# Sums of weight quarters on GpSimd, copies ahead of weighings, and a last product in column halves: a fast matrix product on one core

## Chip, cores, metric

One core of one Trainium2 chip. The metric is the device time of one execution in microseconds (us), as the median of several. The kernel before took 1509.08 us (four runs, 1508.4 to 1509.49), the changed kernel is compared with it below.

## The reference

```python
def reference(x, w):            # x: 8 x 2048 x 2048, w: 2048 x 2048, float32
    cs = np.cumsum(x, axis=1)
    diff = cs - np.concatenate([zeros, cs[:, :-1, :]], axis=1)   # = x up to rounding
    return np.matmul(diff, w).astype(np.float32)
```

The kernel computes x w: 16384 rows by 2048 by 2048. Rows come in tiles of 128, four tiles in a group.

Of the kernel before, what the change touches and what calls it, by code (L numbers as in the profile page):

```python
# [33 lines left out]
def kernel(  # L34
# [6 lines left out]
    nc = tc.nc  # L41
    P = 128
# [7 lines left out]
    NB = 512  # L50
# [3 lines left out]
    ADD = mybir.AluOpType.add  # L54
    SUB = mybir.AluOpType.subtract
    MUL = mybir.AluOpType.mult
    MAX = mybir.AluOpType.max
    AX = mybir.AxisListType
# [75 lines left out]
    def after(engine, ask):  # L134
        if engine in last:
            with tc.issue_after(last[engine].ins):
                said = ask()
        else:
            said = ask()
        last[engine] = said[-1] if isinstance(said, tuple) else said  # L140
        return said


    with tc.tile_pool(name="ring", bufs=7) as ring, tc.tile_pool(
# [97 lines left out]
        def put(c, rows, columns, queue=nc.gpsimd):  # L242
            return queue.dma_start(out2[rows, columns], c)
# [102 lines left out]
        got = {}  # L346
# [130 lines left out]
    def product_in(ps, a, b, first):  # L477
        for k in range(4):
            nc.tensor.matmul(  # L479
                ps, a[k], b[k], start=(first and k == 0), stop=(k == 3), skip_group_check=True  # L480
            )
# [13 lines left out]
    def keep(dst, ps, scale):  # L495
        for c, p in pieces_of(dst, ps):
            after("act", lambda: nc.scalar.activation(c, p, COPY, scale=scale))  # L497
# [12 lines left out]
    def total(dst, p, q, op):  # L510
        after("dve", lambda: nc.vector.tensor_tensor(dst.all, p.all, q.all, op))  # L511

    def less(dst, p, q):
        for k in range(len(dst)):
            after("dve", lambda: nc.vector.tensor_tensor(dst[k], p[k], q[k], SUB))  # L515


    def less_in(Q1, Q2, Q4, t11, t12, t21, t22):
        less(Q1, t12, t11)
        less(Q2, t22, Q1)  # L520
        less(Q4, t21, Q2)

    def less_in3(Q1, Q2, Q4, t11, t12, t21, t22):
        less(t12, t22, t12)

    def new_c(slot):
        return cpool.tile([P, NH], f32, name=f"c{slot}")
# [5 lines left out]
    def fetch_x(t):  # L533
        if t < END:
            came[t], _ = after("sp", lambda: bring(t))

    def weigh(t, slot):
        if t < END:
            xf = came.pop(t)
            m, _ = after("act", lambda: measure(xf, new_c(slot)))  # L540
            got[t] = m, None, xf


    def weigh_in(t, ps):
        if t < END:
            xf = came.pop(t)
            m = small.tile([P, 1], f32, name="m")
            m4 = small.tile([P, 4], f32, name="m4")
            for i in range(4):
                at = ds(i * NB, NB)  # L550
                after(
                    "act",
                    lambda: nc.scalar.activation(  # L553
                        ps[i % 2],
                        xf[:, at],
                        ABS,
                        scale=1.0 / ROW,
                        accum_out=m4[:, i : i + 1],
                    ),
                )  # L560
            after("dve", lambda: nc.vector.tensor_reduce(m, m4, AX.X, ADD))  # L561
            got[t] = m, None, xf

    def scale_of(t):
        if t < END:
            m, _, xf = got[t]
            s, _ = after("dve", lambda: invert(m))
            came[t] = xf, s

# [77 lines left out]
    def group_plain(g, X, Y, Z, V, a, b, c, d):  # L647
        h = g + 2
        ug, uh = unit(g), unit(h)
        A11g, A12g = parts(g)  # L650
        A11h, A12h = parts(h)
        A21g, A22g = parts(g + 1)
        product(X, A11g, B11, True)
        for k in range(3):
            block(B22, 1, 1, k, "act")
        C11g = new_c(a)
        keep(C11g, X, ug)
        for k in range(3, KH):
            block(B22, 1, 1, k, "act" if k < 6 else "dve")
        product(V, A12g, B21, True)  # L660
        product(Y, A11h, B11, True)
        add(C11g, V, ug)
        put(C11g, g, 0)

        less(T3[:2], B22[:2], B12[:2])
        total(S1, A21g, A22g, ADD)
        product(Z, A12h, B21, True)
        weigh(h + 1, d)
        C11h = new_c(b)
        keep(C11h, Y, uh)  # L670
        total(S2, S1, A11g, SUB)
        less(T2[:4], B22[:4], T1[:4])
        scale_of(h + 1)
        vg = unit(g + 1)
        ready(h + 1)
        turn(h + 1)
        fetch_x(h + 4)
        less(T2[4:], B22[4:], T1[4:])
        product(V, S1, T1, True)
        C22 = new_c(d)  # L680
        keep(C22, V, vg)
        less(T3[2:3], B22[2:3], B12[2:3])
        total(S4g, A12g, S2, SUB)
        product(X, S2, T2, False)
        C12g = new_c(c)
        keep(C12g, X, ug)
        total(A21g, A11g, A21g, SUB)
        less(T3[3:], B22[3:], B12[3:])
        product(V, S4g, B22, False)
        A21h, A22h = parts(h + 1)  # L690
        vh = unit(h + 1)
        weigh(g + 4, a)
        product(X, A21g, T3, False)
        total(S1, A21h, A22h, ADD)
        total(S2, S1, A11h, SUB)
        add(C11h, Z, uh)
        put(C11h, h, 0)
        scale_of(g + 4)
        ready(g + 4)
        turn(g + 4)  # L700
        add(C12g, V, ug)
        put(C12g, g, 1)
        fetch_x(g + 5)
        product(Y, S2, T2, False)
        C12h = new_c(a)
        keep(C12h, Y, uh)
        add(C22, X, vg)
        put(C22, g + 1, 1)
        total(S4h, A12h, S2, SUB)
        less(T4, B21, T2)  # L710
        product(Z, S1, T1, True)
        total(A21h, A11h, A21h, SUB)
        weigh(h + 4, b)
        scale_of(h + 4)
        ready(h + 4)
        turn(h + 4)
        fetch_x(h + 5)
        weigh(g + 5, c)
        scale_of(g + 5)
        C22 = new_c(d)  # L720
        keep(C22, Z, vh)
        product(X, A22g, T4, False)
        C21 = new_c(b)
        keep(C21, X, vg)
        ready(g + 5)
        turn(g + 5)
        put(C21, g + 1, 0)
        product(Y, A21h, T3, False)
        add(C22, Y, vh)
        put(C22, h + 1, 1)  # L730
        less_in(*in2)
        less_in3(*in2)
        product(Z, S4h, B22, False)
        add(C12h, Z, uh)
        put(C12h, h, 1)
        fetch_x(g + 8)
        less_in(*in3)
        product(Y, A22h, T4, False)
        C21 = new_c(c)
        keep(C21, Y, vh)  # L740
        put(C21, h + 1, 0)

    def group(g, X, Y, Z, V, a, b, c, d):
# [9 lines left out]
            units[g], units[h] = unit(g), unit(h)  # L753
        u = ug, uh = units.pop(g), units.pop(h)

        C11g = new_c(a)
        keep(C11g, X, ug)
        S3g = sums(g, S4g)
        if second:
            weigh(h + 1, c)  # L760
            ready(h + 1)
            less_in(*in4)
        turn(h + 1)
        fetch_x(h + 4)
        product(Y, A11h, B11, True)
        if second:
            weigh_in(g + 4, V)
        C11h = new_c(b)
        keep(C11h, Y, uh)
        if not second:  # L770
            weigh_in(g + 4, V)
        scale_of(g + 4)
        vg, vh = unit(g + 1), unit(h + 1)
        A21h, A22h = parts(h + 1)
        product(X, S2, T2, False)
        C12g = new_c(c)
        keep(C12g, X, ug)
        one, two, A2 = sums_in(A12g, A12h, S4h, S0)
        one()
        two()  # L780
# [5 lines left out]
        total(A21h, A11h, A21h, SUB)  # L786
        total(S2, S1, A11h, SUB)
        S3h = A21h
        product(X, S3g, T3, False)
        add(C22, X, vg)  # L790
        put(C22, g + 1, 1)
# [11 lines left out]
                ready(h + 4)  # L803

        inner_product(A2, in2, banks, C11g, C11h, *u, between_2)
        if second:
            less_in3(*in3)
            less_in3(*in4)
        total(S4h, A12h, S2, SUB)
        turn(h + 4)  # L810
        put(C11h, h, 0)
# [60 lines left out]
        def four_last():  # L872
            a11, a12, a22, s1, s2, s3, s4 = A4
            Q1, Q2, Q4, t11, Q3, t21, t22 = in4
            C21g, C21h = new_c(b), new_c(c)
            product_in(q, a11, t11, True)
            keep(C21g[:, :NB], q, vg)
            product_in(X[0], a12, t21, False)
            add(C21g[:, :NB], X[0], vg)
            product_in(X[1], s4, t22, False)  # L880
            keep(C21g[:, NB:], X[1], vg)
            product_in(e, s1, Q1, True)
            add(C21g[:, NB:], e, vg)
            keep(C21h[:, NB:], Y[1], vh)
            add(C21h[:, NB:], e, vh)
            product_in(q, s2, Q2, False)
            add(C21g[:, NB:], q, vg)
            put(C21g, g + 1, 0)
            product_in(Y[0], a22, Q4, False)
            keep(C21h[:, :NB], Y[0], vh)  # L890
            product_in(q, s3, Q3, False)
            for n in range(2):
                at = ds(n * NB, NB)
                add(C21h[:, at], q, vh)
                nc.scalar.dma_start(out2[ds((h + 1) * P, P), at], C21h[:, at])

        inner_product(A3, in3, banks, C12g, C12h, *u, between_3)
        put(C12h, h, 1)
# [43 lines left out]
```

## The kernel before: what the change touches

Products are cut by a scheme that uses seven products for eight (with sums of quarters of x and of w) on two levels, in fp16 with a scale a row. TensorE makes products into PSUM banks. ScalarE *weighs* a row tile (sum of absolute values, for its scale), *narrows* it to fp16 (`ready`), and copies the first product of a bank pair out (`keep`). VectorE adds further products (`add`) and makes the sums of x (`sums`, `total`) and of w (`less`). `in2`, `in3`, `in4` are the inner sums of three quarters of w, 12 in `less_in` and 4 in `less_in3` each; they are made once, from the end of the first group (`group_plain`) into the second. `after` keeps the order of instructions on each engine.

```python
def less(dst, p, q):
    for k in range(len(dst)):
        after("dve", lambda: nc.vector.tensor_tensor(dst[k], p[k], q[k], SUB))
# ... end of group_plain (a, b, c, d are slots of the output buffer c) ...
    less(T4, B21, T2)
    product(Z, S1, T1, True)
    weigh(h + 4, b); scale_of(h + 4); ready(h + 4)      # (cut)
    weigh(g + 5, c)
    scale_of(g + 5)
    C22 = new_c(d)
    keep(C22, Z, vh)
    product(X, A22g, T4, False)                         # (cut: keep of X)
    product(Y, A21h, T3, False)
    add(C22, Y, vh)
    less_in(*in2); less_in3(*in2)
    product(Z, S4h, B22, False)
    add(C12h, Z, uh)
    less_in(*in3)
    product(Y, A22h, T4, False)
# ... start of the second group (inside `group`, second == True) ...
    product(X, A11g, B11, True)
    keep(C11g, X, ug)
    S3g = sums(g, S4g)                                  # sums of x, on VectorE
    weigh(h + 1, c); ready(h + 1)
    less_in(*in4)
    product(Y, A11h, B11, True)
    weigh_in(g + 4, V)                                  # in four pieces, waste into PSUM
    keep(C11h, Y, uh)
    product(X, S2, T2, False)
    keep(C12g, X, ug)
    product(Z, S1, T1, True)
    keep(C22, Z, vg)
    # ... inner_product(A2, in2, ...), then:
    less_in3(*in3); less_in3(*in4)
```

## Time and profile before

| | before |
|---|---|
| median time | 1509.08 us |
| TensorE busy, of the span | 1490.6 of 1507.3 us |
| VectorE, ScalarE, GpSimd busy | 1104.4, 864.5, 5.2 us |
| matmuls (all but 64 of 512 columns); one of 512 | 6911; 0.216 us |
| end of the last matmul to the end of the span | 4.9 us |

TensorE is the bound: whatever is gained must come out of the few microseconds in which it stands still. The prediction shows the lines for that.

### The profile page before, as it was taken

Reading aid. Unit: us, or ns where it says so; the run is one execution under the profiler, and the core shown is the slowest. Engines: PE = TensorE matmul, PEld = TensorE weight load, DVE = VectorE, ACT = ScalarE, POOL = GpSimd, SP = SyncE. Lnnn points to the kernel's source line nnn. Section 1 sums busy time; section 2 is a strip of 40 time slices with the busy share of each in tenths; the row PEclk is TensorE's granted clock in tenths of the full one; section 3 lists DMA queues with packets and bytes.
Section 4 is the critical chain, followed back from the end, with each engine's and each line's share of the span. In section 5 each row is a group of like instructions: output and inputs, shape, how many; then the busy total and the mean of one; then the engine's idle time right before and its main releaser. Section 6 shows DMA issues by size and latency. Waiting matters only on the chain.

```text
span 1507.3 us, 19123 instructions
## 1 busy us (share of the span) xinstructions
PE 1490.6 (99%) x6911; PEld 673.8 (45%) x6911; DVE 1104.4 (73%) x2053; ACT 864.5 (57%) x1107; POOL 5.2 (0%) x12
## 2 busy tenths in 40 slices
PE   8999999999999999999999999999999999999998
PEld 3444444444444444444444444444444444444443
DVE  7997777776677676777676776766776767776767
ACT  5875655565655566555656555655555565556551
POOL 0100000000000000000000000000000000000000
PEclk9999999999999999999999999999999999999999
DMA  9988878878978987888789788878788888887772
GB/s 362 351 250 233 236 224 246 234 213 227 235 225 244 224 224 236 215 246 236 210 229 232 230 241 217 235 222 248 216 244 207 236 221 250 232 236 216 223 208 112
DMA packets 322479, 351.50 MB, mean 233 GB/s; under 512 B 266896, under 2 KB 266896, under 8 KB 306512
## 3 DMA queue, kind: packets, MB, share of 16 engines
q1 hardware_dynamic: 321536, 347.92, 81.1%
q0 software_dynamic: 560, 1.84, 0.3%
q8 instruction: 54, 0.88, 0.2%
q10 hardware_dynamic: 288, 0.52, 0.1%
q14 instruction: 41, 0.34, 0.1%
HBM read 150.99 MB, written 134.22 MB: 189 GB/s over the span
## 4 chain that ended last, share of the span: by engine, by line
PE 88%; DVE 1%; DMA 1%; issue 0%; ACT 0%; DVEq 0%; ACTq 0%; SPq 0%
PE b L468 52%; PE b L479 36%; DVE c L502 1%; DMA fin<-in_x_dram 0%; DMA xT<-fin 0%; DVE W L511 0%; ACT b L553 0%; DVE W L515 0%; ACT c L497 0%; DVEq L937 0%; DVE xT L511 0%; DVE s L112 0%; DVE m L111 0%; DVE u L586 0%; DVE m L561 0%
## 5 line engine op out<-in xcount | busy, mean ns | idle before, releaser
L502 DVE SCALAR_TENSOR_TENSOR c<-b,u,c 128x512 f32<-128x512 f32 (+1 forms) x883 | 675.0, 799 | 234.8 <-ACT c L497 112.8
L497 ACT ACTIVATE c<-b,u 128x512 f32<-128x512 f32 x496 | 314.5, 680 | 265.4 <-PE b L468 170.5
L468 PE MATMUL b<-W,xT 128*128 128x512 f16 x2048 | 462.1, 379 | 0.8 <-ACT c L497 0.8
L468 PE MATMUL b<-W,W 128*128 128x512 f16 x1764 | 411.7, 379 | 1.8 <-ACT c L497 1.5
L105 ACT ACTIVATE c<-fin 128x2048 f16<-128x2048 f32 x92 | 175.7, 1910 | 242.4 <-DMA out_dram<-c 220.5
L468 PEld LDWEIGHTS <-xT 128*128 128x128 f16 x2048 | 200.4, 98 | 242.6 <-issue 1.1
L468 PEld LDWEIGHTS <-W 128*128 128x128 f16 x2016 | 197.2, 98 | 240.2 <-issue 2.1
L116 ACT ACTIVATE fin<-fin,s 128x2048 f16<-128x2048 f32 x123 | 246.3, 2002 | 93.8 <-issue 50.8
L479 PEld LDWEIGHTS <-W 128*128 128x128 f16 x1560 | 152.1, 98 | 187.5 <-issue 2.5
L479 PE MATMUL b<-W,W 128*128 128x512 f16 x810 | 220.0, 379 | 1.0 <-DVE c L502 1.0
L479 PE MATMUL b<-W,xT 128*128 128x512 f16 x720 | 180.0, 379 | 0.0
L479 PE MATMUL b<-inner,W 128*128 128x512 f16 x660 | 176.2, 379 | 0.0
L479 PEld LDWEIGHTS <-xT 128*128 128x128 f16 x960 | 93.9, 98 | 113.3
L561 DVE TENSOR_REDUCE m<-m 128x1 f32<-128x4 f32 x29 | 4.6, 157 | 106.7 <-ACT b L553 106.7
L553 ACT ACTIVATE b<-fin 128x512 f32<-128x512 f32 x116 | 67.8, 585 | 14.5 <-DMA fin<-in_x_dram 14.5
L468 PE MATMUL b<-W 128*128 128x512 f16 x252 | 75.0, 379 | 0.0
L511 DVE TENSOR_TENSOR W<-W,xT 128x1024 f16<-128x1024 f16 x122 | 68.2, 559 | 3.2
L511 DVE TENSOR_TENSOR W<-xT,W 128x1024 f16<-128x1024 f16 x122 | 67.5, 553 | 0.0
L479 PE MATMUL b<-inner,xT 128*128 128x512 f16 x240 | 61.6, 379 | 0.0
L233 PE MATMUL b<-wb,xP 128*128 128x512 bf16 x240 | 55.4, 383 | 5.9 <-ACT wb L216 4.8
L511 DVE TENSOR_TENSOR W<-xT,xT 128x1024 f16<-128x1024 f16 (+1 forms) x92 | 54.8, 596 | 0.0
L111 DVE TENSOR_SCALAR m<-m 128x1 f32<-128x1 f32 x124 | 18.5, 149 | 34.6 <-ACT c L105 33.5
(54 smaller groups left out, 457.9 us busy)
## 6 DMA issues: line engine op xcount, KB each, us to landing
out_dram<-c SPq DMA_DIRECT2D x247, 512.0 KB, 3.1
fin<-in_x_dram SPq DMA_DIRECT2D x123, 1024.0 KB, 5.5
W<-in_w_dram SPq DMA_DIRECT2D x32, 512.0 KB, 9.6
W<-in_x_dram SPq DMA_DIRECT2D x16, 256.0 KB, 7.4
xT<-fin SPq DMA_TRANSPOSE x184, 5.2
out_dram<-o POOLq DMA_DIRECT2D x7, 256.0 KB, 3.9
out_dram<-o SPq DMA_DIRECT2D x7, 256.0 KB, 4.1
xP<-in_x_dram SPq DMA_DIRECT2D x1, 1024.0 KB, 5.1
```

Source lines behind the costliest of these rows:

```text
L105: return m, nc.scalar.activation(waste.bitcast(f16), xf, ABS, scale=1.0 / ROW, accum_out=m)
L111: nc.vector.tensor_scalar(m, m, TINY, None, MAX)
L116: return xh, nc.scalar.activation(xh, xf, COPY, scale=s)
L233: lambda: nc.tensor.matmul(ps[r][n], xP[:, r, ko, :], wb[h, ko][:, ds(n * NB, NB)], start=(ko == 0), stop=(ko == KO - 1),),
L468: nc.tensor.matmul(ps[n], a[k], b[k][:, n, :], start=(first and k == 0), stop=(k == KH - 1), skip_group_check=True,)
L479: nc.tensor.matmul(ps, a[k], b[k], start=(first and k == 0), stop=(k == 3), skip_group_check=True)
L497: after("act", lambda: nc.scalar.activation(c, p, COPY, scale=scale))
L502: "dve", lambda: nc.vector.scalar_tensor_tensor(c, p, scale, c, MUL, ADD)
L511: after("dve", lambda: nc.vector.tensor_tensor(dst.all, p.all, q.all, op))
L553: lambda: nc.scalar.activation(ps[i % 2], xf[:, at], ABS, scale=1.0 / ROW, accum_out=m4[:, i : i + 1],),
L561: after("dve", lambda: nc.vector.tensor_reduce(m, m4, AX.X, ADD))
```

## The change

Its intent: take the inner sums of in3 and in4 off VectorE, let ScalarE's copies, on which TensorE waits, go ahead of weighings, and shorten what lies behind the last matmul.

```diff
-    def less(dst, p, q):
+    def less(dst, p, q, engine="dve"):
+        by = {"dve": nc.vector, "pool": nc.gpsimd}[engine]
# group_plain
+        C22 = new_c(d)
+        keep(C22, Z, vh)
         weigh(g + 5, c)
         scale_of(g + 5)
-        C22 = new_c(d)
-        keep(C22, Z, vh)
...
+        less_in(*in4, engine="pool")
         less_in(*in2)
         less_in3(*in2)
...
-        less_in(*in3)
         product(Y, A22h, T4, False)
+        less_in3(*in4, engine="pool")
+        less_in(*in3, engine="pool")
+        less_in3(*in3, engine="pool")
# group, second: weigh(h + 1) becomes weigh_in(h + 1, V), ahead of keep(C11g, X);
#   weigh_in(g + 4, V) goes behind keep(C11h, Y) and keep(C12g, X);
#   less_in(*in4), less_in3(*in3), less_in3(*in4) go away;
#   the sum over the four pieces of weigh_in moves into scale_of (cut)
# four_last: products in the order a11, a12, s2, s1, s4, s3, then
+            for at, ps, queue in (one, Y[0], nc.sync), (two, X[0], nc.scalar):
+                product_in(ps[:, at], a22, [b[:, at] for b in Q4], ps is X[0])
+                add(C21h[:, at], ps[:, at], vh)
+                out_of(C21h, h + 1, at, queue)     # a store of 256 columns
```

More of the change, by code (lines that the diff above doesn't have):

```diff
@@ L511, in total, with less_in, less_in3 @@
         after("dve", lambda: nc.vector.tensor_tensor(dst.all, p.all, q.all, op))
-    def less(dst, p, q):
+    def less(dst, p, q, engine="dve"):
+        by = {"dve": nc.vector, "pool": nc.gpsimd}[engine]
         for k in range(len(dst)):
-            after("dve", lambda: nc.vector.tensor_tensor(dst[k], p[k], q[k], SUB))
-    def less_in(Q1, Q2, Q4, t11, t12, t21, t22):
-        less(Q1, t12, t11)
-        less(Q2, t22, Q1)
-        less(Q4, t21, Q2)
-    def less_in3(Q1, Q2, Q4, t11, t12, t21, t22):
-        less(t12, t22, t12)
+            after(engine, lambda: by.tensor_tensor(dst[k], p[k], q[k], SUB))
+    def less_in(Q1, Q2, Q4, t11, t12, t21, t22, engine="dve"):
+        less(Q1, t12, t11, engine)
+        less(Q2, t22, Q1, engine)
+        less(Q4, t21, Q2, engine)
+    def less_in3(Q1, Q2, Q4, t11, t12, t21, t22, engine="dve"):
+        less(t12, t22, t12, engine)
     def new_c(slot):
@@ L560, in weigh_in @@
                 )
-            after("dve", lambda: nc.vector.tensor_reduce(m, m4, AX.X, ADD))
-            got[t] = m, None, xf
+            got[t] = m, m4, xf
     def scale_of(t):
         if t < END:
-            m, _, xf = got[t]
+            m, of_parts, xf = got[t]
+            if of_parts is not None:
+                after("dve", lambda: nc.vector.tensor_reduce(m, of_parts, AX.X, ADD))
             s, _ = after("dve", lambda: invert(m))
@@ L754, in group @@
         u = ug, uh = units.pop(g), units.pop(h)
+        if second:
+            weigh_in(h + 1, V)
         C11g = new_c(a)
@@ L759, in group @@
         if second:
-            weigh(h + 1, c)
+            scale_of(h + 1)
             ready(h + 1)
-            less_in(*in4)
+            product(Y, A11h, B11, True)
+            C11h = new_c(b)
+            keep(C11h, Y, uh)
         turn(h + 1)
         fetch_x(h + 4)
-        product(Y, A11h, B11, True)
-        if second:
+        if not second:
+            product(Y, A11h, B11, True)
+            C11h = new_c(b)
+            keep(C11h, Y, uh)
             weigh_in(g + 4, V)
-        C11h = new_c(b)
-        keep(C11h, Y, uh)
-        if not second:
-            weigh_in(g + 4, V)
-        scale_of(g + 4)
+            scale_of(g + 4)
         vg, vh = unit(g + 1), unit(h + 1)
@@ L777, in group @@
         keep(C12g, X, ug)
+        if second:
+            weigh_in(g + 4, V)
         one, two, A2 = sums_in(A12g, A12h, S4h, S0)
@@ L788, in group @@
         S3h = A21h
+        if second:
+            scale_of(g + 4)
         product(X, S3g, T3, False)
@@ L805, in group @@
         inner_product(A2, in2, banks, C11g, C11h, *u, between_2)
-        if second:
-            less_in3(*in3)
-            less_in3(*in4)
         total(S4h, A12h, S2, SUB)
@@ L875, in four_last, with out_of @@
             C21g, C21h = new_c(b), new_c(c)
+            def out_of(c, t, at, queue):
+                queue.dma_start(out2[ds(t * P, P), at], c[:, at])
             product_in(q, a11, t11, True)
@@ L879, in four_last @@
             add(C21g[:, :NB], X[0], vg)
+            out_of(C21g, g + 1, ds(0, NB), nc.sync)
+            product_in(q, s2, Q2, False)
+            keep(C21g[:, NB:], q, vg)
+            product_in(e, s1, Q1, True)
+            one, two = (ds(n * NB // 2, NB // 2) for n in range(2))
+            keep(C21h[:, two], Y[0][:, two], vh)
+            keep(C21h[:, NB:], Y[1], vh)
             product_in(X[1], s4, t22, False)
-            keep(C21g[:, NB:], X[1], vg)
-            product_in(e, s1, Q1, True)
             add(C21g[:, NB:], e, vg)
-            keep(C21h[:, NB:], Y[1], vh)
             add(C21h[:, NB:], e, vh)
-            product_in(q, s2, Q2, False)
-            add(C21g[:, NB:], q, vg)
-            put(C21g, g + 1, 0)
-            product_in(Y[0], a22, Q4, False)
-            keep(C21h[:, :NB], Y[0], vh)
-            product_in(q, s3, Q3, False)
-            for n in range(2):
-                at = ds(n * NB, NB)
-                add(C21h[:, at], q, vh)
-                nc.scalar.dma_start(out2[ds((h + 1) * P, P), at], C21h[:, at])
+            add(C21g[:, NB:], X[1], vg)
+            out_of(C21g, g + 1, ds(NB, NB), nc.sync)
+            product_in(q, s3, Q3, False)
+            keep(C21h[:, one], q[:, one], vh)
+            add(C21h[:, NB:], q, vh)
+            add(C21h[:, two], q[:, two], vh)
+            out_of(C21h, h + 1, ds(NB, NB), nc.scalar)
+            for at, ps, queue in (one, Y[0], nc.sync), (two, X[0], nc.scalar):
+                product_in(ps[:, at], a22, [b[:, at] for b in Q4], ps is X[0])
+                add(C21h[:, at], ps[:, at], vh)
+                out_of(C21h, h + 1, at, queue)
         inner_product(A3, in3, banks, C12g, C12h, *u, between_3)
```

## The prediction

> **What bounds the kernel now.** I read the page first (busy shares, slices, groups), then the waits of TensorE alone, then busy time by window around each wait, then the instructions in order of time around the second group and at the end.
>
> ```profile
> PE 1490.6 (99%) x6911; PEld 673.8 (45%) x6911; DVE 1104.4 (73%) x2053; ACT 864.5 (57%) x1107; POOL 5.2 (0%) x12
> PE  8999999999999999999999999999999999999998
> L515 DVE TENSOR_TENSOR inner<-W,inner 128x512 f16<-128x512 f16 x18 | 6.3, 419 | 0.0
> ```
>
> TensorE is busy for 1490.6 of 1507.3 us at full clock, with 6911 matmuls. The chain of waits shows 64 matmuls in 13.81 us, so one costs 0.216 us, and 6911 x 0.216 = 1491 us. Neither the count of products nor their cost changes. All that can be won lies in the 16.7 us where TensorE is idle: some 9 us in the first 60 us (loads and casts of w, untouched), about 5 us behind the last matmul, and single holes. The waits of TensorE name the holes:
>
> ```profile
> PE b L468 <- ACT c L497: 2.3, 3, 1.3
> PE b L479 <- DVE c L502: 1.0, 3, 0.5
> PE b L468 <- DVE W L511: 0.3, 1, 0.3
> ```
>
> The columns are the total, the count and the longest, in us. Windows give the size and place of each hole (first PE figure against the window's length):
>
> ```profile
> 115.00:120.00 5.00, 3.48 (x16) 1.43 (x15) 1.95 (x5) 4.24 (x7) 0.00 (x0) 1.00 0.75 180
> 138.00:142.00 4.00, 3.22 (x16) 1.40 (x15) 2.70 (x11) 4.00 (x10) 0.00 (x0) 1.00 0.70 126
> 157.00:160.00 3.00, 2.80 (x14) 1.21 (x13) 2.96 (x7) 1.19 (x2) 0.00 (x0) 1.00 0.72 138
> 1499.00:1502.00 3.00, 2.50 (x12) 1.07 (x11) 2.07 (x3) 1.30 (x3) 0.00 (x0) 1.00 0.31 130
> ```
>
> So 1.52, 0.78, 0.20 and 0.50 us, 3.0 us together. Two more, 0.30 us near 96 us and 0.33 us near 651 us, are not addressed by the change. Between 160 us and 1500 us TensorE runs without a hole but the one at 651 us, so what is saved before 160 us reaches the end unless a load arrives too late. The end, in order of time:
>
> ```profile
> 1501.40 0.38 PE L479 MATMUL b<-W,W 128*128 128x512 f16 x1 [0.50 <-DVE c L502]
> 1501.83 0.59 PE L479 MATMUL b<-W,W 128*128 128x512 f16 x2
> 1502.53 1.41 DVE L502 SCALAR_TENSOR_TENSOR c<-b,u,c 128x512 f32<-128x512 f32 x2 [1.18 <-PE b L479]
> 1503.32 1.00 ACTq L895 DMA_DIRECT2D out_dram<-c  x2
> ```
>
> The last matmul ends at 1502.4, two adds of 512 columns end at 1503.94, two stores of 256 KB land 2.4 us after issue, at about 1506.4, and the program closes at 1507.3.
>
> **What the Trainium skill says.** (1) "GPSIMD Engine Reference", section 3.1, gives about 2.6 cycles an element at 1.2 GHz for a two-input elementwise sum, and says VectorE is about twice as fast. My estimate from that page: 512 x 2.6 / 1.2 = 1.11 us a sum, 1.2 with dispatch. The trace before has no elementwise work of this kind on GpSimd, so no run shows it yet; on VectorE the same sum takes 0.42 us alone and 0.35 us in a row (8 in 2.77 us). (2) "SBUF — State Buffer", section "Who interferes with whom": a VectorE instruction with two SBUF inputs contends with a GpSimd instruction that reads SBUF, and the later one blocks for a whole instruction. GpSimd is idle there in the trace before, so this too is unseen. VectorE's adds of a PSUM bank into c have one SBUF tensor and should be free of it. (3) "TensorE: Matmul & The Clock Gate", section "Wait — 56ns, not 53.3ns?": columns / 2.4 GHz plus 2.5 ns. That is 215.8 ns for 512 columns, which the trace confirms (13.81 / 64), and 109 ns for 256. (4) "DMA: Bandwidth & Descriptors", section "Anatomy of one DMA": about 2.0 us fixed, the rest by bytes. The trace's 2.4 to 2.7 us for stores of 256 and 512 KB at the end agrees roughly: smaller pieces save tenths, not microseconds.
>
> **The change part by part.**
>
> *The copy ahead of the weighing in the first group.* At 115.76 ScalarE weighs a tile (1.91 + 0.19 us), having waited 1.94 us for its load, and only then, at 117.67, copies Z out; the product of Z with B22 waits for this until 118.39 and 118.97. Now the copy comes first: it can run at 113.8, in the time in which ScalarE waited for the load. It takes 2 x 0.63 us and is done by 115.1, before TensorE is there at 116.9. The store that frees its slot was issued at 109.7 and lands after about 3.1 us, at 112.8. Gain 1.52 us.
>
> *The weighings in the second group.* Before, ScalarE weighs h+1 (1.9 us), narrows it (2.0 us) and weighs g+4 in four pieces (2.4 us) before two due copies; the third product into X starts 0.78 us late. Before that ScalarE sits idle for 3.9 us at 127 to 130.8, waiting for a VectorE scalar that stands behind sums of quarters. Now the weighing of h+1 moves into that idle stretch, and the copies of Y and X go ahead of the weighing of g+4. I followed the new order with the durations above: X is copied by about 136, TensorE needs it at 137.9. Gain 0.78 us.
>
> *Sums to GpSimd.* 12 + 4 for in4 and 12 + 4 for in3 are 32 sums, 32 x 0.35 = 11.2 us off VectorE: 4.0 us at 126.4, 4.1 us at 134.2 and 2.8 us at 153.4. The last stood in front of the sums of the third product, which gave the 0.20 us hole at 159. Gain 0.20 us directly; the other sums only relieve VectorE. On GpSimd they take 32 x 1.2 = 38 us (estimate). They may start when T4 begins to be ready, at 106.6, and in3 is due at about 155 (156.9 before, less the shift): 48 us are there.
>
> *The end.* The wait of 0.50 us falls: it came because bank q was added by VectorE just before it was refilled, and the new order puts two products and a ScalarE copy between. The last product in two halves is 8 x 109 ns = 0.87 us against 4 x 216 = 0.86: nothing lost. Behind it VectorE has a queue of its own: I counted an add of 512 columns at 0.66 us spacing and 256 columns at about 0.40 (an estimate: the halved column part plus the fixed part of the 1272 and 746 ns rows). From the last full product (ending about 1500.9 on the old scale) come 0.66 + 3 x 0.40, starting only when older adds are done, so VectorE ends at about 1503.2, not 1503.94. It, not TensorE, bounds this stretch, so the whole 0.50 us is not worth another 0.50. The last store has 128 KB instead of two of 256 KB together: some 0.4 us less to move, at the 390 to 416 GB/s that the end shows. So 0.7 + 0.4 = 1.1 us for the end, the 0.50 us included.
>
> Sum: 1.52 + 0.78 + 0.20 + 1.1 = 3.6 us; 1508.95 - 3.6 = 1505.3 us with nothing going wrong.
>
> **The rivals.**
>
> *The port becomes the bound.* If each GpSimd sum shuts out VectorE's two-input sums, the two form one queue: from 107 to 155 us VectorE has some 18 us of them (8 x 0.61 for T4, 16 x 0.35 for in2, sums of x for the rest), and 18 + 38 = 56 us is more than the 48 that are there. T4 is the sharp spot: it is finished at 110.9 and TensorE needs its last piece at 113, so two GpSimd sums in between cost nothing, and four cost some 3 us. Then in3 could also be late by a few us. Speaking for it: the page's wording and the tightness. Against: VectorE loses 11.2 us of work, and GpSimd must itself wait for pieces of T4. Time: 1508 to 1517.
>
> *The gain is eaten by loads.* What is won before 160 us brings TensorE closer to transfers; the 0.33 us hole at 651 us, whose chain goes back over a load of 6.29 us, says that slack there is not endless. It would give back at most a microsecond or so: 1506 to 1507.
>
> *The end gains nothing.* If VectorE's queue or the fixed part of the store sets the end, as I half expect, only about 0.3 us of the 1.1 come: 1506.1.
>
> I take some port contention as likely but mostly absorbed: 0.5 us on the 1505.3.
>
> **Range and chances.** The certain part, holes whose releaser is simply moved away, is about 2.5 us; the end is 0.3 to 1.6. All well gives 1504.5 to 1505.5; the port rival has perhaps one chance in four and pulls upwards. I say 1505.8, with 1503.5 to 1511.0. Two per cent are 30 us: there are not 30 us of idle TensorE to win, and even the port rival's worst case loses under 10. So within 2% is nearly certain.
>
> **What would show it right or wrong.** Right: no TensorE waits on ScalarE copies between 115 and 142, GpSimd with 44 instructions and some 40 us busy between 107 and 155, and the same product starting about 2.5 us earlier at 200 us. The last VectorE add ends about 3.2 us earlier than before. Wrong: VectorE's two-input sums longer than 0.42 and 0.68 us between 107 and 155; TensorE waiting on VectorE W at T4, or on GpSimd in the third product; or a hole moved to the next group, where loads come late.

## More of the kernel before

Single runs of one kernel differ by up to about 2 us (1508.86 to 1510.66 in nine runs of the kernel before on one chip).

One more view matters for what follows: VectorE, in order of time, where the sums of in2 and in3 are made. The columns are the start, the time of the whole row, engine, line, operation, and the count.

```profile
119.70 1.42 DVE L515 TENSOR_TENSOR W<-W 128x512 f16<-128x512 f16 x4
...
123.72 1.42 DVE L515 TENSOR_TENSOR W<-W,W 128x512 f16<-128x512 f16 x4
125.06 1.40 DVE L502 SCALAR_TENSOR_TENSOR c<-b,u,c 128x512 f32<-128x512 f32 x2
...
130.65 0.68 DVE L511 TENSOR_TENSOR W<-xT,xT 128x1024 f16<-128x1024 f16 x1
```

The 16 sums of in2 run from 119.70 to 125.06, 0.34 us from one to the next. VectorE then has no gap up to the sums of x at 130.65, which the third product of the second group needs.

## The result and the profile after

The changed kernel takes 1524.99 us (1524.4 to 1525.32, four runs) against 1509.08: 15.9 us more, ratio 1.0105 with an interval of 1.0088 to 1.0123. Ratios here are the mean time of one kernel's fast runs over that of the other's of the same rounds, so not quite the ratio of the medians. The prediction said 1505.8, with 1503.5 to 1511.0.

TensorE's waits, changed kernel (total, times, longest, in us):

```profile
PE b L468 <- DVE W L511: 14.4, 2, 14.1
...
PE b L479 <- DVE c L502: 2.1, 1, 2.1
...
PE b L468 <- ACT c L497: 0.9, 2, 0.7
```

One wait makes nearly all of it. In order of time it reads so, VectorE, GpSimd and TensorE of the changed kernel:

```profile
111.82 0.68 DVE L511 TENSOR_TENSOR xT<-xT,xT 128x1024 f16<-128x1024 f16 x1
...
107.92 8.94 POOL L516 TENSOR_TENSOR inner<-W 128x512 f16<-128x512 f16 x4 [42.50 <-PE b L468]
...
121.57 1.41 DVE L502 SCALAR_TENSOR_TENSOR c<-b,u,c 128x512 f32<-128x512 f32 x2
...
122.89 4.81 DVE L516 TENSOR_TENSOR W<-W 128x512 f16<-128x512 f16 x4
...
126.09 5.21 POOL L516 TENSOR_TENSOR W<-W,W 128x512 f16<-128x512 f16 x4
...
137.96 5.24 DVE L516 TENSOR_TENSOR W<-W,W 128x512 f16<-128x512 f16 x4
143.12 1.40 DVE L502 SCALAR_TENSOR_TENSOR c<-b,u,c 128x512 f32<-128x512 f32 x2
...
144.68 1.18 DVE L511 TENSOR_TENSOR W<-xT,xT 128x1024 f16<-128x1024 f16 x1
...
147.47 1.04 PE L468 MATMUL b<-W,W 128*128 128x512 f16 x2 [14.14 <-DVE W L511]
```

The rows 111.82 and 107.92 belong to the stretch before, in which T4 is made (see the failed step below). The same 16 sums of in2 that took 5.4 us now take from 122.89 to 143.12, 20.2 us, one in about 1.3 us, which is the pace of GpSimd's sums beside them (4 in 5.2 us). VectorE's sums of x behind them come 14 us late, and TensorE waits 14.1 us. The two adds at 143.12, which read one operand from PSUM, take 1.40 us as ever, though GpSimd is at work. After the long wait the first matmuls come 0.43 us apart; the 32 up to 155.70 take 8.2 us where 6.9 would do, 1.3 us more.

The end, from the start of the last product of eight to the end of the span, takes 14.8 us (from 1508.75) where it took 15.2 (from 1492.11).

### The profile page after: what moved, and what is told of

It is laid out like the page before. It is cut to its first block, busy times and chain, and to the rows that moved or that the text cites. A ratio compares the mean times of both kernels' runs of the same rounds, so it can differ in the third digit from the quotient of the medians.

```text
span 1523.5 us, 19159 instructions
## 1 busy us (share of the span) xinstructions
PE 1493.7 (98%) x6909; PEld 674.9 (44%) x6915; DVE 1113.7 (73%) x2024; ACT 865.3 (57%) x1114; POOL 50.3 (3%) x44
## 4 chain that ended last, share of the span: by engine, by line
PE 89%; DVE 2%; ACT 1%; issue 0%; DVEq 0%; ACTq 0%
PE b L468 53%; PE b L479 35%; DVE W L516 1%; DVE c L502 1%; DVE inner L516 0%; DVE W L511 0%; ACT c L497 0%; DVE xT L511 0%; ACT b L554 0%; ACT c L105 0%; DVEq L955 0%; DVE m L111 0%; DVE s L112 0%; DVE u L588 0%; DVE m L568 0%
## 5 line engine op out<-in xcount | busy, mean ns | idle before, releaser
L502 DVE SCALAR_TENSOR_TENSOR c<-b,u,c 128x512 f32<-128x512 f32 (+2 forms) x885 | 675.4, 798 | 238.8 <-ACT c L497 118.1
L497 ACT ACTIVATE c<-b,u 128x512 f32<-128x512 f32 (+1 forms) x497 | 315.1, 679 | 276.9 <-PE b L468 171.4
L479 PE MATMUL b<-inner,xT 128*128 128x512 f16 (+1 forms) x244 | 61.6, 376 | 0.0
```

The costliest lines, as they stand in the source:

```text
L479: nc.tensor.matmul(ps, a[k], b[k], start=(first and k == 0), stop=(k == 3), skip_group_check=True)
L497: after("act", lambda: nc.scalar.activation(c, p, COPY, scale=scale))
L502: "dve", lambda: nc.vector.scalar_tensor_tensor(c, p, scale, c, MUL, ADD)
```

## The experiments

Each was timed beside the kernel before on the same chip; times are medians. All results are correct.

**e1_sums_on_dve**: the change with the 32 sums left on VectorE, in their old places.

```diff
-        less_in(*in4, engine="pool")
-        less_in3(*in4, engine="pool"); less_in(*in3, engine="pool"); less_in3(*in3, engine="pool")
+        less_in(*in3)                          # before product(Y, A22h, T4)
+            less_in(*in4)                      # second group, behind ready(h + 1)
+            less_in3(*in3); less_in3(*in4)     # behind inner_product(A2, ...); places cut
```

> The whole change, but all 32 sums of quarters stay on VectorE in the places that they had before. Theory (port): GpSimd's sums hold up VectorE's sums one for one, and all of the loss is theirs. Then no TensorE wait above 1 us is left after 100 us, and the time is 1506.5 to 1508.2 us, a little under the kernel before. Rival (order of copies and weighings): the 2.1 us wait on VectorE c near 164 us and part of the 14 us stay, and the time is 1511 us or more.

Measured: 1511.35 against 1509.24 us (ratio 1.0014, 1.0001 to 1.0027). So most of the loss is GpSimd's, but the expectation missed: what is left of the change does not gain, it loses 2.1 us. That is the time that the rival forecast (1511 us or more), and a part of its waits is there: 2.0 of the 14 us on VectorE W, and 1.1 us on VectorE c. The waits of e1:

```profile
PE b L468 <- DVE W L511: 2.3, 2, 2.0
PE b L479 <- DVE c L502: 1.6, 3, 1.1
...
PE b L468 <- ACT c L497: 0.9, 3, 0.5
```

And e1 in order of time:

```profile
117.43 1.26 ACT L497 ACTIVATE c<-b,u 128x512 f32<-128x512 f32 x2 [3.04 <-PE b L468]
...
118.58 1.91 ACT L105 ACTIVATE c<-fin 128x2048 f16<-128x2048 f32 x1
...
120.61 0.15 DVE L111 TENSOR_SCALAR m<-m 128x1 f32<-128x1 f32 x1 [8.31 <-ACT c L105]
...
122.20 1.42 DVE L516 TENSOR_TENSOR W<-W 128x512 f16<-128x512 f16 x4
```

The copy that was to run at about 114 starts at 117.43. The weighing behind it ends later than before, VectorE waits for the weighing's result (8.31 us), and its sums of in2 begin at 122.20 instead of 119.70. The wait that left the copy came back as one of 2.0 us behind the sums of x.

**e2_sums_on_gpsimd_only**: the kernel before with nothing but the 32 sums moved, as in the change.

> The kernel before with nothing but the 32 sums moved to GpSimd. Theory (port): 16 sums of in2 on VectorE at about 1.3 us spacing instead of 0.35, a TensorE wait of 12 to 16 us on VectorE W near 133 us, time 1521 to 1527 us. Rival (the new order of weighings is needed for the loss): below 1515 us.

Measured: 1522.62 against 1509.24 us (ratio 1.009). The time is as expected and the in2 sums run from 120.20 to 140.06; the TensorE wait on them is 9.5 us, shorter than expected.

```profile
144.42 1.03 PE L468 MATMUL b<-W,W 128*128 128x512 f16 x2 [9.51 <-DVE W L511]
```

Most of the rest is matmuls that come 0.43 us apart: the 32 behind this wait take 1.3 us too long, as in the changed kernel, and 16 from 118.89 on take 5.5 us where the kernel before needs 3.8 (from 118.39). The two waits for ScalarE's copies are 0.8 us longer together. GpSimd's part costs 13.4 us; with e1's 2.1 that makes 15.5 of the 15.9 us, if the two simply add.

**e3_end_only**: the kernel before with nothing but the new `four_last`.

> The kernel before with nothing but the new last product. From the profile after: the stretch from the last full product of eight to the end was 14.75 us against 15.2 us before, so 1508.5 us, 0.4 to 0.6 us less than before. My prediction's step said 1.1 us less (1508.0).

Measured: 1509.0 against 1509.24 us (ratio 0.9999, 0.9985 to 1.0012). A gain of 0.2 us lies within what the runs can tell. In its trace the wait of 0.50 us at the end is gone, but from the end of the last matmul to the end of the span it is 5.0 us, where it was 4.9.

**e4_gpsimd_halves**: the changed kernel with each GpSimd sum cut into two of 256 columns.

```diff
+            for at in (ds(0, 256), ds(256, 256)):
+                after("pool", lambda: by.tensor_tensor(dst[k][:, at], p[k][:, at], q[k][:, at], SUB))
```

> The changed kernel, but each GpSimd sum is cut into two of 256 columns. If the two engines take turns by whole instructions, a sum on VectorE now waits for one of about 0.6 us instead of 1.2: VectorE's 16 sums of in2 at about 0.65 to 0.75 us spacing, 11 us instead of 20, the TensorE wait falls from 14 us to about 4 us, and the time is 1512 to 1517 us. If they share the port's bandwidth, or GpSimd simply goes first by priority, the spacing stays near 1.3 us and the time at 1523 us or more.

Measured: 1536.62 us, 27 us above before. The time is that of the second forecast (1523 us or more), but neither has the mechanism: VectorE does not wait for half a sum, nor at the old spacing; it does not get in at all.

```profile
122.13 31.00 DVE L521 TENSOR_TENSOR W<-W 128x512 f16<-128x512 f16 x4
153.05 0.74 DVE L521 TENSOR_TENSOR W<-W,W 128x512 f16<-128x512 f16 x2
```

```profile
116.71 10.08 POOL L519 TENSOR_TENSOR inner<-W,inner 128x256 f16<-128x256 f16 x16
126.74 5.07 POOL L519 TENSOR_TENSOR W<-W,W 128x256 f16<-128x256 f16 x8
```

The first fence is VectorE, the second GpSimd, both of e4. GpSimd's sums follow each other at 0.63 us, undisturbed. The first of VectorE's sums is recorded from 122.13 to 152.12, past 47 GpSimd sums; the last of them ends at 151.84. After that VectorE's sums are back at 0.34 us. TensorE waits 27.5 us.

**e5_idle_sums, e6_idle_memsets, e7_idle_copies**: the kernel before, none of its work moved, and GpSimd doing work that nobody uses.

```diff
+        after("pool", lambda: nc.gpsimd.tensor_copy(in4[2][0], T4[7][:, 1, :]))
+        for k in range(16):        # e6: 30 memsets; e7: 22 tensor_copy of T4[4 + k % 4][:, 1, :]
+            after("pool", lambda: nc.gpsimd.tensor_tensor(
+                in4[2][k % 4], T4[4 + k % 4][:, 1, :], T4[4 + k % 4][:, 0, :], SUB))
         less_in(*in2)
```

> The kernel before, all its own sums left on VectorE, plus 17 GpSimd instructions whose result nobody uses (a copy that waits for the last piece of T4, then 16 two-input sums of 512 columns), overwriting a buffer that VectorE fills later. Theory (read port): VectorE's in2 sums go at about 1.3 us each while GpSimd runs, TensorE waits 8 to 15 us on VectorE W near 130 us, time 1518 to 1526 us, though nothing was moved. Rival (the loss comes from data of in3 or in4 being late, or from the changed order): 1509 to 1511 us.

> As e5_idle_sums, but 30 GpSimd memsets of the same 512 columns in place of the 16 sums: GpSimd writes and does not read. Theory (read port): VectorE's in2 sums stay at 0.35 us and the time within 1 us of before, 1508.5 to 1510.5 us. Rival (any GpSimd work in SBUF, its writes included, holds VectorE up): in2 sums longer than 0.5 us, time above 1512 us.

> As e5_idle_sums, but 22 GpSimd copies of 512 columns, which read one input. Theory (read port, lock of whole instructions, GpSimd's instructions back to back): VectorE's two-input sums are held as well, at least 0.5 us each or shut out until the copies end, time 1511 to 1520 us. If only GpSimd's two-input sums hold them, the time is 1508.5 to 1510.5 us.

Measured on one chip, with before at 1509.7: e5 1524.41 us (ratio 1.0098), e6 1510.16 us (1.0004, 0.9988 to 1.0021), e7 1514.46 us (1.0032, 1.0017 to 1.0047). The beginning of in2 on VectorE and GpSimd beside it, first e5, then e6, then e7:

```profile
120.29 5.32 DVE L515 TENSOR_TENSOR W<-W 128x512 f16<-128x512 f16 x4
...
120.29 20.54 POOL L733 TENSOR_TENSOR inner<-W 128x512 f16<-128x512 f16 x16 [7.70 <-issue]
```

```profile
119.94 1.42 DVE L515 TENSOR_TENSOR W<-W 128x512 f16<-128x512 f16 x4
...
112.21 14.05 POOL L733 MEMSET inner<- 128x512 f16 x30
```

```profile
119.36 6.30 DVE L515 TENSOR_TENSOR W<-W 128x512 f16<-128x512 f16 x4
125.59 0.74 DVE L515 TENSOR_TENSOR W<-W,W 128x512 f16<-128x512 f16 x2
...
112.09 12.30 POOL L733 COPY inner<-W 128x512 f16<-128x512 f16 x22
```

e5 has the whole loss without a single sum moved; its TensorE wait:

```profile
PE b L468 <- DVE W L511: 14.8, 1, 14.8
```

So neither late results of in3 or in4 nor the new order are needed for it. Memsets, which only write, change nothing: four of VectorE's sums in 1.42 us, with GpSimd busy all through. Copies, which read one input, shut VectorE out until they end at 124.4, as the halves did. All three expectations held. It is GpSimd's reads of SBUF that hold VectorE's two-input sums.

**e8_free_slot, e9_free_slot_all**: is the late copy of e1 due to its slot? In e8 the kernel before with the new end takes the copy ahead of the weighing, but into slot c; e9 does the same to e1, so it has the second group's new order as well.

```diff
-        weigh(g + 5, c)
-        scale_of(g + 5)
-        C22 = new_c(d)
+        C22 = new_c(c)
         keep(C22, Z, vh)
+        weigh(g + 5, b)
+        scale_of(g + 5)
...
-        C21 = new_c(c)
+        C21 = new_c(d)
```

> The kernel before with the new end, and with the first group's copy of Z ahead of the weighing, but into the slot c, whose store was issued some 7 us earlier, while the weighing writes its waste to b. Theory (the copy waited for the store of its slot, issued at 110.7 and landed 7.4 us later): the copy starts at about 114.5, the hole of 1.5 us near 117 is gone and VectorE's in2 sums start no later than before; time 1507.0 to 1508.0 us. Rival (the copy waits for TensorE, as the profile names it): it stays at 117 or later and the time at 1509 us or more.

> e1_sums_on_dve with the same free slot: the whole change without GpSimd, with the copy not held by its store. If the order of the second group is harmless once VectorE's in2 sums start in time, the wait of 2.0 us near 134 goes and about 1 us near 149 stays or shrinks: 1507.5 to 1509.0 us, no better than e8_free_slot. If the new order of the second group gains its 0.8 us, it is 0.5 us or more below e8_free_slot.

Measured, with before at 1509.87: e8 1508.55 us (ratio 0.9994, 0.998 to 1.0007), e9 1509.28 us (0.9998, 0.9986 to 1.0011). The copy now starts at 114.07 in e8, so it was the slot: the profile's name for its releaser, TensorE, was wrong, for TensorE had ended that product at 111. In the changed kernel the store out of slot d was issued at 110.68, and the two stores issued from 107 to 120 took these times to land, of which the 7.4 is this one's:

```profile
DMA to landing us min/median/max: 3.3/5.3/7.4
```

110.68 and 7.4 make 118.1, which is when the copy began (118.11). But at most part of the 1.5 us came out as time: e8's 1508.55 misses its forecast (1507.0 to 1508.0), e9's 1509.28 both of its own (1507.5 to 1509.0, or 0.5 below e8), and neither is told from the kernel before. TensorE's busy time by window in e8; behind the window and its length come the busy times of TensorE, its weight loads, VectorE, ScalarE and GpSimd, each with a count, then the clock, the DMA share and GB/s:

```profile
115.00:120.00 5.00, 5.00 (x25) 2.25 (x23) 2.01 (x6) 4.37 (x6) 0.00 (x0) 1.00 0.77 199
120.00:130.00 10.00, 10.00 (x48) 4.53 (x47) 10.00 (x29) 2.37 (x3) 0.00 (x0) 1.00 1.05 321
130.00:136.00 6.00, 5.27 (x25) 2.25 (x24) 5.22 (x15) 4.90 (x5) 0.00 (x0) 1.00 0.76 254
136.00:145.00 9.00, 7.77 (x37) 3.42 (x35) 7.66 (x22) 8.05 (x16) 0.00 (x0) 1.00 0.64 171
```

The hole near 117 is closed, but 0.73 us opens at 131, where there was none, and 1.23 instead of 0.78 at 139. The third busy time shows why: VectorE is busy 10.00 of 10 us from 120 to 130, as before. TensorE came earlier and found VectorE not ready. In e9 the hole at 139 is gone, but there are 0.74 us at 132 and one of 1.08 at 147.

**e10_sums_later, e11_sums_later_all**: e8 and e9 with `less_in(*in3)` moved behind `sums(g, S4g)`, on VectorE.

> e8_free_slot with one more move on VectorE alone: the 12 sums of in3 come behind the four sums of x that open the second group, not before them. Theory (VectorE, not a copy, is what bounds 120 to 136 us once the hole near 117 is closed): the hole of 0.73 us between 130 and 136 us goes, and the one of 1.23 us behind it shrinks to 0.8 us or less; time 1506.8 to 1508.0 us. Rival (the sums are due at once and the hole only moves): 1508.3 us or more.

> e9_free_slot_all with the same move, so the whole change without GpSimd, with the free slot and with the sums of in3 behind those of x. If the weighing that stands ahead of the copy of Z delays VectorE's adds (the wait of about 1.1 us near 149 us in e1 and e9), that wait stays and the time is 0.2 to 1.0 us above e10_sums_later; if it was only VectorE's lateness, the wait goes and the time is at or below e10_sums_later.

Measured, with before at 1509.5: e10 1508.97 us (ratio 0.9997, 0.9983 to 1.0011), a miss, in the range of its rival; e11 1507.2 us (ratio 0.9985, 0.9973 to 0.9998), 2.3 us below before. TensorE's waits between 100 and 200 us, e10 and then e11:

```profile
PE b L468 <- ACT c L497: 2.1, 2, 1.9
```

```profile
PE b L479 <- DVE c L502: 0.8, 1, 0.8
```

In e10 VectorE is in time, and the wait has moved to ScalarE, whose old order puts a weighing, a narrowing and a second weighing in front of the copy of X. The first weighing also starts late:

```profile
131.09 1.91 ACT L105 ACTIVATE c<-fin 128x2048 f16<-128x2048 f32 x1 [2.44 <-DMA out_dram<-c]
```

It writes its waste to a slot whose store, issued at 125.72, landed at 131.06. The change's weighing in pieces writes to PSUM and needs no slot, so e10 and e11 do not tell the order from this hold. With the change's order, e11 has one wait of 0.8 us left in this stretch. Its wait at 147 in e9 was thus partly VectorE's lateness (1.08 to 0.80 us). e11 is the change without GpSimd, with another slot and with one block of sums moved on VectorE; it is the fastest kernel here.

## Why the prediction was wrong, step by step

*What bounds the kernel* was right: TensorE, at 0.216 us a matmul, with the waits named. The class, within 2%, was right too. The number was not.

*Sums to GpSimd: the failed step.* I called the port a rival with one chance in four and wrote "some port contention as likely but mostly absorbed: 0.5 us". It is 13.4 us alone (e2), and the whole of it appears with GpSimd doing idle sums (e5: 14.7 us). The prediction's own first sign of being wrong came: sums of in2 of 1.37 us and sums of x of 1.63 us, in place of 0.42 and 0.68. My duration of a GpSimd sum was right: 1.15 us as recorded, 1.11 from start to start when alone, against 1.11 to 1.2 forecast. What I did not do is the sum that follows at once from the page I quoted, the Trainium skill's "SBUF — State Buffer", section "Who interferes with whom": if VectorE's 16 sums of in2 wait for one GpSimd sum each, they last, as an estimate, 16 x 1.2 = 19 us instead of 5.4, and the sums of x, due just behind them, are 14 us late. Measured 20.2 us and 14.1 us. I had written the two engines' work as one queue and asked whether 56 us fit into 48; the damage is not in the total but in the order: GpSimd's sums, not urgent, go one for one ahead of VectorE's urgent ones. I also looked for it at T4, where VectorE was not held: its eight sums took 4.89 us from 107.00 (before: 4.90). There GpSimd seems to have been the one that waited: its first sum, recorded from 107.92, took 5.60 us and ended at 113.52, 1.02 us after VectorE's run of two-input sums ended at 112.50. In e2 the distance is 1.02 us too, in e4 0.53 for half a sum. No run separates this from some other cost of a first sum. And the rival's worst case, 1517, allows for 8 us where the one wait is 14.1; it left out the 1.3 us of slow matmuls after it and the 2.1 us wait further on. My range ended at 1511, below that worst case.

*The copy in the first group.* Forecast: 1.52 us. The slot's store landed after 7.4 us, not the 3.1 us that the profile's page gives as the median of all stores; the copy was held to 118.1 (in the changed kernel), the hole shrank only to 0.95 us, and the later weighing then held up VectorE (e1, e8). I took a median where the one store in question, issued 0.4 us behind a load of 1 MB, should have been looked up.

*Holes do not add.* I summed 1.52, 0.78 and 0.20 as if each were free time. e8, e9 and e10 show that VectorE and ScalarE stood right behind each of these waits: closing the first gave 0.73 us at the next engine. All together, with one more move, gave 2.3 us (e11) of the 3.6 forecast, and no smaller set that was run gave a gain clear of the noise.

*The order in the second group.* Forecast 0.78 us. It shows only with VectorE in time: e11 against e10 gains 1.8 us, in part perhaps because a weighing no longer waits for its slot; e9 against e8 loses 0.7, of which the spread of single runs is a good part.

*The end.* Forecast 1.1 us; 0.45 us in the trace, 0.2 in time (e3), not told from zero. The 0.50 us wait did go. The 0.4 us for smaller stores did not come: 3.4 us from the last add to the end of the span in both kernels.

*What stays open.* Why sums of 512 columns on GpSimd let VectorE in once each, while copies of 512 and sums of 256 columns, back to back, shut it out altogether, and whether VectorE's own run at T4 shut GpSimd out in the same way. No run here tells.

## What to carry to other kernels

Work moved to GpSimd is not out of VectorE's way if it reads SBUF while VectorE has two-input SBUF instructions on a short path: count at least one GpSimd instruction of waiting for each of them (in e4 and e7 it was the rest of GpSimd's run), and ask which of VectorE's results is due first. Before a wait is booked as a gain, ask which engine stands next behind it; here the time fell clear of the noise only when three were moved together. And a buffer that is to be reused earlier has to be free earlier: look up the landing of that one store.

## What the Trainium skill lacked or had wrong

- "SBUF — State Buffer", "Who interferes with whom", says that the later instruction blocks until the first one finishes. It agrees on who is hit (e6: memsets leave VectorE at 0.34 us a sum; e5 and e7: reads do not; an add with one PSUM operand kept 1.40 us for two). It lacks that the wait can last past many instructions that start after the one that waits: 30.0 us and 47 GpSimd sums of 256 columns (e4), 5.0 us of copies (e7).
- The same page calls the pair an exclusive lock for the whole instruction. With sums of 512 columns the two engines got through one each in 1.30 us, less than the 1.11 and 0.34 us that they take alone. That need not contradict the page: some of each may pass without the port, and no run shows how much.
- "GPSIMD Engine Reference", section 2.1, gives about 6 us for the first call of a freshly loaded kernel, counted from the instruction MODIFY_POOL_CONFIG. In e5 that instruction stands at 112.63 and the first sum at 120.29, with no wait that the profile shows: 7.7 us. In the changed kernel it stands at 65.5, 42 us before the first sum, so the 5.60 us of that sum are no test of the figure.
- "DMA: Bandwidth & Descriptors", "Anatomy of one DMA", gives about 2.0 us fixed and the rest by bytes, for DMAs that GpSimd issues; those here go out on the sync and scalar queues. The skill has no time for a store that stands behind a load on the same queue: one of 512 KB, issued 0.4 us behind a load of 1 MB, landed after 7.4 us.
